# Delta heads traced with a tile between producer and reader, an adaLN closing in two jobs, one pool of four PSUM banks

## The chip, the cores and the metric

One core of a Trainium2 chip runs the kernel. The metric is the device time of one execution in microseconds (us); lower is better. A time "before" is the median of three runs; a profile is one execution taken by the hardware profiler.

## What is computed

A trunk of two layers over 512 latent and 256 context tokens of width 2048. Each layer modulates and normalises its input with shift, scale and gate vectors that come from `silu(c) @ ada_w + ada_b` (adaLN, 2048 to 6144, once for the latents' condition and once for the context's), runs one combined input projection of 6480 columns, and feeds three head groups: four retention heads, four gated Delta heads, eight latent-attention heads. All are gated, joined by one output projection and added to the residual.

```python
h = rmsnorm(x, norm_w[i]) * (1.0 + scale[:, None]) + shift[:, None]
zl = split_cols(h @ w_in[i], IN_SPLITS)
# gated DeltaNet, per head of 128:
qkv = silu(centred_dwconv(concat([q, k, v]), conv_w))   # 5 taps
q = l2norm(q) * 128 ** -0.5;  k = l2norm(k)
# S_t = a_t (I - b_t k_t k_t^T) S_{t-1} + b_t k_t v_t^T,  o_t = S_t^T q_t, both directions
```

## The kernel before

Tokens lie along the free dimension: a tile is 128 features by 768 tokens, context first (256), then latents (512). A projection of 128 columns (`proj`, L290, through `proj_in`, L363) takes 16 row blocks of 128; the weights come from HBM in four loads, are split into a high and a low float32r part (`wh` on ACT, L227; `wl` on VectorE, L228; four buffers each of four row blocks), and every row block gives three products, each one matmul over the latents (`zl`, L284) and one over the context (`zc`, L286). The result is evicted from PSUM by `evac` (L369): the context half on VectorE (L371), the latent half on ACT (L372).

A layer has three phases. Phase A makes all input projections and runs the Delta and retention heads. Phase B is the attention, phase C the output projection. Which instruction stands where on an engine is fixed when the program is built: the order in the source is a priority, and the framework lays each engine's queue by that priority and by its own estimate of when operands and buffers are ready. The chip then works each queue in order. So a reader may be placed too early for the chip, and then its engine waits.

`gdn_head(h, gs)` (L756) is one Delta head. `conv_in` (L737) takes a projection, evicts it to `cz`, makes the five-tap convolution `cy` (an ACT copy, L744, and eight steps on VectorE, L751) and a SiLU (`ce`, L392 to L396, L400). It does this for the query (`qT`), the key (`kr`) and the value (`vT`). Behind the query come its squares (`lsq`, ACT, L763) and the sums of these by small matmuls (`ss`, L767). Behind the key come the transposes by TensorE (`knp`, `turn`, L661), the norm's rsqrt from sums of squares (`token_rstd`, L650), the scaled key `kn` (L664), and its transposes back (`ktp`) that are copied to `kT`. The value is turned in `vnp` (L787). In the source each of these readers stands right behind what it reads: `ss` behind the query's squares, then the key's `conv_in`, then `knp`, `ktp`, then the value's `conv_in`, then `vnp`. In head 0 the gate's projection (`gate`, L618) stands between the value and `vnp`. Then follow the decay masks, the triangular inverse (`vtp`, `xp`, `rp`, `xrp`) and the scan of six steps in both directions (`chain`, from L908), and `out_norm` (`osq`, `ot`).

The head is a long row of dependent steps. What covers them is a list `fill` of other projections (latents for the attention `cq`, `ckv`, gates `gg`, `mg`, retention inputs `rr`), of which so many are emitted behind each head (`nf`, L1057), with lower priority for coming later. The order by hand is in these lines:

```python
fill = cq + gg[1:2] + ckv + gg[2:3] + rr[0] + gg[3:] + rr[1] + rr[2] + rr[3] + mg
nf = [7, 6, 4, 5, 3, 3, 4, 4]
for i, n in enumerate(nf):
    (gdn_head if i < 4 else ret_head)(*((i, gs) if i < 4 else (i - 4,)))
    for f in fill[sum(nf[:i]):sum(nf[:i + 1])]:
        f()
```

The query, key and value of head 0 are projected before phase A (`first_groups`, L319), so its three `conv_in` find their sums ready.

The adaLN vectors that are not needed at the start are made in 64 jobs, one in the middle of each projection of phase A of layer 0 and in its phase C (`ada_job`, L510). A job loads a part of `ada_w`, scales it on ACT (`ada_p`, L474) and sums it on GpSimd (`ada_a`, L476; eight additions of 128x512). After every four jobs, the next job closes a group (`ada_close`, L492): eight small matmuls into `ada_z` (L497), a copy to `ada_e` by ACT (L501), and behind it at once four matmuls that read `ada_e` into `ada_q` (L504) and an addition on VectorE (L505).

PSUM has three kinds of tiles: `pz` (tag `z`, one bank, 3 of them: all `zl`, `zc`, `ada_z`, `ada_q`, the attention's transposes `ptp` and values `vz`), `pm` (tag `m`, two banks, 2 of them) and `pc` (tag `ch`, one bank, 1 of them: the scan's first direction `chain`, the attention's sums `oacc` and the first adaLN sums).

Of the kernel before, what the change touches and what calls it, by code (L numbers as in the profile page):

```python
# [11 lines left out]
F32 = mybir.dt.float32  # L12
# [8 lines left out]
P = 128  # L21
# [11 lines left out]
C_GDN = 2048  # L33
# [68 lines left out]
def trunk(  # L102
# [16 lines left out]
    ps = ctx.enter_context(tc.tile_pool(name="ps", bufs=1, space=PSUM))  # L119
    dr = ctx.enter_context(tc.tile_pool(name="dr", bufs=1, space=DRAM))  # L120

    def pz(name="z"):
        return ps.tile([P, 512], F32, name=name, tag="z", bufs=3)

    def pm(name="m"):
        return ps.tile([P, 1024], F32, name=name, tag="m", bufs=2)

    def pc(name="ch"):
        return ps.tile([P, 512], F32, name=name, tag="ch", bufs=1)

    def lslot(name, dt=F32R):
        return lp.tile([P, NT], dt, name=name, tag="L")
# [3 lines left out]
    def w_(tag, name, dt=F32, n=NT):  # L136
        return wk.tile([P, n], dt, name=name, tag=tag, bufs=BUFS[tag])

    mk = lambda name: w_("t", name)
# [61 lines left out]
    def col_params(parts, n, name, alloc=None, queue=None):  # L201
        st = mk("pst")
        V.memset(st[:, :P], 0.0)
        o = 0
        for ap in parts:
            r = ap.shape[0] // P
            (queue or dma)(out=st[o:o + r, :P], in_=rows(ap))
            o += r
        p_ = pz("pst_ps")
        T.transpose(p_[:, :P], st[:, :P], ident)  # L210
        d = alloc(name)[:, :n] if alloc else fixed(n)
        V.tensor_copy(d, p_[:, :n])
        return d
# [149 lines left out]
    def proj_in(l, c0, hs, need_ctx):  # L363
        if (l, c0) in ready:
            return ready.pop((l, c0))
        segs, m = in_segs(l, c0)
        return proj(segs, hs, m, need_ctx, True)

    def evac(dst, zl, zc, m=P, scale=1.0):  # L369
        if zc is not None:  # L370
            V.tensor_scalar(out=dst[:m, 0:NX], in0=zc[:m, :NX], scalar1=scale, scalar2=None, op0=ALU.mult)  # L371
        S.activation(out=dst[:m, NX:NT], in_=zl[:m], func=AF.Copy, scale=scale)  # L372
# [25 lines left out]
    def silu_mul(dst, src, e):  # L398
        sigmoid(e, src)
        V.tensor_tensor(out=dst, in0=src, in1=e, op=ALU.mult)  # L400
# [30 lines left out]
    def ada_scale(l, n0, n):  # L431
        if 16 <= n0 < 32:
            k0 = n0 - 16
            V.tensor_scalar(out=s1[l][:, k0:k0 + n, :], in0=ada_t[l][:, n0:n0 + n, :],
                            scalar1=1.0, scalar2=None, op0=ALU.add)
            V.tensor_tensor(out=s1[l][:, k0:k0 + n, :], in0=s1[l][:, k0:k0 + n, :],
                            in1=par[l, 0][:, 48 + k0:48 + k0 + n].unsqueeze(2).to_broadcast([P, n, 2]), op=ALU.mult)
# [24 lines left out]
    ada_state = {}  # L462
# [20 lines left out]
    def ada_run(job):  # L483
        l, s, qd = job
        if qd == 0:
            ada_accs.append(wk.tile([P, 2, 256], F32, name="ada_a", tag="ada_a", bufs=3))
        for i in range(2):
            ada_quad(l, s, qd + i, ada_accs[-1])
        if qd and s % 2:
            ada_state[1] = (l, 2 * s - 2)  # L490

    def ada_close(l, n0):  # L492
        z = pz("ada_z")[:, :256]
        for i, acc in enumerate(ada_accs):
            for v in range(2):
                g = 2 * i + v
                T.matmul(z[32 * g:32 * g + 32], lhsT=ones[:, :32], rhs=acc[:, v], start=True, stop=True,  # L497
                         tile_position=(0, 32 * g))
        ada_accs.clear()
        e = wp.tile([P, 256], F32, name="ada_e", tag="ada_e", bufs=2)  # L500
        S.copy(e, z)  # L501
        q = pz("ada_q")
        for j in range(2):
            T.matmul(q[:, 4 * j:4 * j + 4], lhsT=e[:, j * P:(j + 1) * P], rhs=sel4, start=True, stop=True)  # L504
        V.tensor_tensor(out=ada_t[l][:, n0:n0 + 4, :].rearrange("p (i j) v -> p i j v", j=2),  # L505
                        in0=q[:, :8].rearrange("p (j i v) -> p i j v", j=2, i=2),
                        in1=par[l, 0][:, n0:n0 + 4].rearrange("p (i j) -> p i j", j=2).unsqueeze(3).to_broadcast([P, 2, 2, 2]), op=ALU.add)
        ada_scale(l, n0, 4)

    def ada_job():  # L510
        if 1 in ada_state:
            ada_close(*ada_state.pop(1))
        job = next(ada_jobs, None)
        if job:
            ada_run(job)
# [91 lines left out]
    def phase_a(l, hs):  # L607
        last = l == DEPTH - 1
        parB = par[l, 1]
        if True:  # L610
# [7 lines left out]
            def gate(c0, j):  # L618
                lo_ctx = not last
                zl, zc = proj_in(l, (c0), hs, lo_ctx)  # L620
                z, e = ev("gz"), ev("ge")
                lo = 0 if lo_ctx else NX
                evac(z, zl, zc)
                silu_mul(z[:, lo:], z[:, lo:], e[:, lo:])
                dma(out=gate_d[l][j][:, lo:], in_=z[:, lo:])
# [24 lines left out]
            def token_rstd(src, c0, sq, fill_v):  # L650
                ss, y, t = tiny("nss"), tiny("nry"), tiny("nrt")
                for n in range(c0, NCH):
                    S.activation(out=sq[:, n * P:(n + 1) * P], in_=src[:, n * P:(n + 1) * P], func=AF.Square,
                                 accum_out=ss[:, n:n + 1])
                fill_v(ss[:, c0:])
                rsqrt(ss[:, c0:], y[:, c0:], t[:, c0:])
                return ss

            def turn(dst, src, c0):
                for n in range(c0, NCH):  # L660
                    T.transpose(dst[:, n * P:(n + 1) * P], src[:, n * P:(n + 1) * P], ident)  # L661

            def scale_tokens(dst, src, r, c0):
                V.tensor_tensor(out=c6(dst)[:, c0:], in0=c6(src)[:, c0:],  # L664
                                in1=r[:, c0:].unsqueeze(2).to_broadcast([P, NCH - c0, P]), op=ALU.mult)
# [71 lines left out]
            def conv_in(dst, c0, grp, need_ctx):  # L737
                zl, zc = proj_in(l, c0, hs, need_ctx)
                z = ev("cz")
                lo = 0 if need_ctx else NX  # L740
                evac(z, zl, zc)
                y = mk("cy")
                w = lambda j: parB[:, 12 * j + grp:12 * j + grp + 1]
                S.activation(out=y[:, lo:NT], in_=z[:, lo:NT], func=AF.Copy, scale=w(2))  # L744
                for j in (0, 1, 3, 4):
                    o = j - 2
                    for a, b in ((0, NX), (NX, NT)):
                        if a < lo:
                            continue
                        a_, b_ = max(a, a - o), min(b, b - o)  # L750
                        V.scalar_tensor_tensor(out=y[:, a_:b_], in0=z[:, a_ + o:b_ + o], scalar=w(j),  # L751
                                               in1=y[:, a_:b_], op0=ALU.mult, op1=ALU.add)
                e = mk("ce")
                silu_mul(dst[:, lo:NT], y[:, lo:NT], e[:, lo:NT])

            def gdn_head(h, gs):  # L756
                be, gcol, egl, ekd, nbe = gs
                qT = pt("qT")
                qlo = NX if last else 0
# [1 line left out]
                qv = tiny("qv")  # L761
                sq = mk("lsq")
                S.activation(out=sq[:, qlo:NT], in_=qT[:, qlo:], func=AF.Square)  # L763
                m = pm("ss")
                c0 = qlo // P
                for n in range(c0, NCH):
                    T.matmul(m[:, n:n + 1], lhsT=sq[:, n * P:(n + 1) * P], rhs=ones[:, 0:1], start=True, stop=True)  # L767
                V.tensor_scalar(out=qv[:, c0:], in0=m[:, c0:NCH], scalar1=EPS, scalar2=EPS * HD, op0=ALU.add, op1=ALU.mult)
                kr = mk("kr")
                conv_in(kr, C_GDN + 512 + h * P, 4 + h, True)  # L770
                kT, kn = pt("kT"), pt("kn")
                m = pm("knp")
                turn(m, kr, 0)
                r = token_rstd(m, 0, kr, lambda ss: V.tensor_scalar(out=ss, in0=ss, scalar1=EPS, scalar2=None, op0=ALU.add))
                scale_tokens(kn, m, r, 0)
                m = pm("ktp")
                turn(m, kn, 0)
                S.copy(kT, m[:, :NT])
                vT = mk("vT")
                conv_in(vT, C_GDN + 1024 + h * P, 8 + h, True)  # L780
                if h == 0:
                    gate(C_GDN + 1536, 4)

                vn = pt("vn")
                m = pm("vnp")
                for n in range(NCH):
# [261 lines left out]
            gs = kr_ab()  # L1048
# [4 lines left out]
            gg = [lambda h=h: gate(C_GDN + 1536 + h * P, 4 + h) for h in range(4)]  # L1053
            mg = [lambda j=j: gate(C_MG + j * P, 8 + j) for j in range(8)]
            mg.insert(6, lambda: pair_groups(l, (C_MG + 6 * P, C_MG + 7 * P), hs, not last))
            fill = cq + gg[1:2] + ckv + gg[2:3] + rr[0] + gg[3:] + rr[1] + rr[2] + rr[3] + mg
            nf = [7, 6, 4, 5, 3, 3, 4, 4]  # L1057
            for i, n in enumerate(nf):
                (gdn_head if i < 4 else ret_head)(*((i, gs) if i < 4 else (i - 4,)))
                for f in fill[sum(nf[:i]):sum(nf[:i + 1])]:  # L1060
                    f()

    def phase_b(l):
# [313 lines left out]
```

## Time and profile before

| | us |
|---|---|
| median of three runs | 3215.6 |
| the three runs | 3215.6, 3217.71, 3211.18 |
| the profiled execution | 3222.98 |
| its span, first to last instruction | 3221.2 |
| TensorE busy in it | 3053.8 |
| VectorE / ACT / GpSimd busy in it | 2031.1 / 1657.0 / 697.1 |

PE is TensorE, DVE VectorE, ACT ScalarE, POOL GpSimd, SP the engine that issues the transfers; L661 is line 661 of the kernel. In a row of waits the instruction left of `<-` waited for the one right of it. In a timeline a bracket gives the idle time of that engine before the instruction and what ended it. A row by stretches gives a stretch, its length, each engine's busy time with its number of instructions, TensorE's granted clock as a share of 2.4 GHz, the transfers' share and GB/s.

### The profile page before, as it was taken

The page shows a single profiled execution, that of the slowest core. Times are in us where ns is not written, and L with a number is a line of the kernel's source. Part 1 is how long each engine was busy: PE and PEld are TensorE (multiplying, and loading weights), DVE is VectorE, ACT ScalarE, POOL GpSimd, SP SyncE. Part 2 cuts the span into 40 slices and gives each one's busy share as a digit, 9 for nine tenths or more (in the row PEclk, how much of TensorE's full clock was granted, in tenths as well). Part 3 has the DMA queues.
Part 4 walks back from the last instruction along what each step waited for, and adds up shares of the span by engine and source line. Part 5 has one row for each costly group of instructions (what it writes and reads, how often), then busy time and mean ns, then how long its engine had stood idle before and what let it go on. Part 6 is the DMA issues. An engine that isn't in the chain of part 4 may idle for free.

```text
span 3221.2 us, 50805 instructions
## 1 busy us (share of the span) xinstructions
PE 3053.8 (95%) x18925; PEld 2589.3 (80%) x18925; DVE 2031.1 (63%) x3524; ACT 1657.0 (51%) x3492; POOL 697.1 (22%) x487
## 2 busy tenths in 40 slices
PE   6998989989889999999999999999999999999998
PEld 3576878878778878899888888888898888888887
DVE  3269568477577566766763355867585767766644
ACT  3266555654555656544677645442424245544534
POOL 0036344443443544000268700000000000000000
PEclk8999999989999999999999999999999999999999
DMA  8763433423424545512465542322323256512444
GB/s 286 257 193 115 122 103 99 133 66 92 134 79 141 159 144 159 159 48 60 136 216 164 160 122 66 98 72 61 102 58 99 74 149 186 147 54 62 134 118 129
DMA packets 496655, 399.22 MB, mean 124 GB/s; under 512 B 45367, under 2 KB 433047, under 8 KB 496407
## 3 DMA queue, kind: packets, MB, share of 16 engines
q1 hardware_dynamic: 496083, 395.87, 41.5%
q8 instruction: 148, 2.42, 0.3%
q14 instruction: 101, 0.82, 0.1%
q0 software_dynamic: 96, 0.02, 0.0%
q10 hardware_dynamic: 227, 0.08, 0.0%
HBM read 340.90 MB, written 54.97 MB: 123 GB/s over the span
## 4 chain that ended last, share of the span: by engine, by line
PE 53%; POOL 2%; ACT 2%; DMA 2%; DVE 2%; issue 1%; SPq 0%; ACTq 0%; POOLq 0%; DVEq 0%
PE zl L284 21%; PE zlc L284 7%; PE zc L286 5%; PE vz L267 4%; PE sc L1157 3%; POOL ada_a L476 2%; PE oacc L1216 2%; PE zt L275 2%; PE zlc L286 1%; PE ptp L1209 1%; PE racc L1037 1%; DMA araw<-in_ada_w_dram 1%; PE f L284 1%; ACT ada_p L474 1%; DMA gb<-g_d 0%
## 5 line engine op out<-in xcount | busy, mean ns | idle before, releaser
L476 POOL TENSOR_TENSOR ada_a<-ada_a,ada_p 128x512 f32<-128x512 f32 x480 | 695.1, 1448 | 1144.8 <-ACT ada_p L474 1098.7
L228 DVE TENSOR_TENSOR wl<-raw,wh 128x512 fp32r<-128x512 f32 x632 | 486.3, 771 | 421.2 <-ACT wh L227 333.1
L227 ACT CAST wh<-raw 128x512 fp32r<-128x512 f32 x632 | 377.8, 605 | 562.0 <-PE zc L286 208.3
L284 PE MATMUL zl<-hh,wh 128*128 128x512 f32 (+1 forms) x1440 | 581.4, 404 | 1.9 <-ACT hh L227 1.8
L284 PE MATMUL zl<-hl,wh 128*128 128x512 f32 (+1 forms) x1440 | 581.3, 404 | 1.0 <-DVE hl L228 1.0
L284 PE MATMUL zl<-hh,wl 128*128 128x512 f32 (+1 forms) x1440 | 581.3, 404 | 0.0
L474 ACT ACTIVATE ada_p<-araw,const_f 128x256 f32<-128x256 f32 x960 | 423.4, 501 | 64.7 <-DMA araw<-in_ada_w_dram 41.3
L284 PEld LDWEIGHTS zl<-hh,wh 128*128 128x128 f32 (+1 forms) x1440 | 274.0, 190 | 64.9 <-issue 3.8
L284 PEld LDWEIGHTS zl<-hh,wl 128*128 128x128 f32 (+1 forms) x1440 | 274.1, 190 | 58.6 <-issue 1.1
L284 PEld LDWEIGHTS zl<-hl,wh 128*128 128x128 f32 (+1 forms) x1440 | 273.8, 190 | 58.6 <-DVE hl L228 2.5
L286 PE MATMUL zc<-hh,wh 128*128 128x256 f32 (+1 forms) x960 | 279.6, 291 | 6.1 <-ACT ce L372 4.9
L286 PE MATMUL zc<-hl,wh 128*128 128x256 f32 (+1 forms) x960 | 277.9, 289 | 0.0
L286 PE MATMUL zc<-hh,wl 128*128 128x256 f32 (+1 forms) x960 | 277.8, 289 | 0.0
L286 PEld LDWEIGHTS zc<-hh,wh 128*128 128x128 f32 (+1 forms) x960 | 183.8, 191 | 14.6 <-ACT ce L372 6.7
L286 PEld LDWEIGHTS zc<-hh,wl 128*128 128x128 f32 (+1 forms) x960 | 184.3, 192 | 3.4 <-issue 2.9
L286 PEld LDWEIGHTS zc<-hl,wh 128*128 128x128 f32 (+1 forms) x960 | 184.5, 192 | 2.6 <-issue 0.8
L284 PE MATMUL zlc<-mh,wl 128*128 128x512 f32 x448 | 178.6, 399 | 0.0
L284 PE MATMUL zlc<-mh,wh 128*128 128x512 f32 x448 | 178.0, 397 | 0.0
L284 PE MATMUL zlc<-ml,wh 128*128 128x512 f32 x448 | 177.3, 396 | 0.0
L751 DVE SCALAR_TENSOR_TENSOR cy<-cz,const_f,cy 128x511 f32<-128x511 f32 (+3 forms) x176 | 141.8, 859 | 17.8 <-ACT cy L744 17.3
L284 PEld LDWEIGHTS zlc<-mh,wh 128*128 128x128 f32 x448 | 84.9, 189 | 20.4 <-ACT ada_p L474 0.8
L284 PEld LDWEIGHTS zlc<-ml,wh 128*128 128x128 f32 x448 | 84.8, 189 | 19.0
(1250 smaller groups left out, 6419.3 us busy)
## 6 DMA issues: line engine op xcount, KB each, us to landing
raw<-in_w_in_dram SPq DMA_DIRECT2D x368, 256.0 KB, 3.6
araw<-in_ada_w_dram SPq DMA_DIRECT2D x256, 256.0 KB, 3.4
raw<-in_w_out_dram SPq DMA_DIRECT2D x144, 256.0 KB, 3.8
ar<-in_ada_w_dram SPq DMA_DIRECT2D x128, 256.0 KB, 5.1
x_d<-xt SPq DMA_DIRECT2D x32, 384.0 KB, 3.6
raw<-in_w_in_dram SPq DMA_DIRECT2D x72, 128.0 KB, 3.4
ret_d<-rw SPq DMA_DIRECT2D x20, 384.0 KB, 2.8
rz<-ret_d SPq DMA_DIRECT2D x20, 384.0 KB, 3.5
```

The costliest lines, as they stand in the source:

```text
L227: S.copy(hi, src)
L228: V.tensor_tensor(out=lo, in0=src, in1=hi.bitcast(F32), op=ALU.subtract)
L267: T.matmul(z[:, 256 * i:256 * i + 256], lhsT=x_[:, (j + i) * P:(j + i + 1) * P], rhs=w, start=first and k == 0 and i == 0, stop=end and k ...
L275: T.matmul(z, lhsT=w, rhs=xx[:, a:b], start=own and first and k == 0, stop=own and last and k == nk - 1)
L284: T.matmul(zl[:m], lhsT=w, rhs=xx[:, NX:], start=st, stop=sp)
L286: i = T.matmul(zc[:m, :NX], lhsT=w, rhs=xx[:, :NX], start=st and zc_open, stop=sp and zc_open)
L474: S.activation(out=pr[:, v], in_=raw[:, i, :], func=AF.Copy, scale=cs32[:, 2 * k + v:2 * k + v + 1])
L476: G.tensor_tensor(out=acc, in0=acc, in1=pr, op=ALU.add)
L751: V.scalar_tensor_tensor(out=y[:, a_:b_], in0=z[:, a_ + o:b_ + o], scalar=w(j), in1=y[:, a_:b_], op0=ALU.mult, op1=ALU.add)
L1037: T.matmul(acc[:, :NL], lhsT=a[:, sl], rhs=b[:, :NL], start=st and i == 0, stop=sp and i == NCH - 1)
L1157: T.matmul(m[:, po:po + n], lhsT=a[:, qs], rhs=b[:, ko:ko + n], start=i == 0, stop=i == len(ops) - 1)
L1216: T.matmul(acc[:, os], lhsT=a[:, sl], rhs=b[:, js], start=j == 0 and n == 0, stop=j == nk - 1 and n == 2)
```

## The change

Three edits. First, `gdn_head` takes one more argument, `between`, and its readers move: the key's `conv_in` stands before the query's `ss`, the value's `conv_in` before the key's `knp`, and `between()`, one projection, before `ktp`. In head 0 it is the gate that stood in the head before; in heads 1 to 3 it is the first of the head's own fills (one of `ckv`, then two of the retention inputs), which are one fewer behind the head. Second, the closing of an adaLN group is cut in two: `ada_close` ends with the copy to `ada_e`, and the matmuls into `ada_q` with what follows are `ada_turn`, called at the beginning of the next `ada_job`. Third, `pc` draws on the tag `z`, which has four banks in place of three and one.

```diff
     def pz(name="z"):
-        return ps.tile([P, 512], F32, name=name, tag="z", bufs=3)
+        return ps.tile([P, 512], F32, name=name, tag="z", bufs=4)
...
     def pc(name="ch"):
-        return ps.tile([P, 512], F32, name=name, tag="ch", bufs=1)
+        return ps.tile([P, 512], F32, name=name, tag="z", bufs=4)
...
         S.copy(e, z)
+        return l, n0, e
+
+    def ada_turn(l, n0, e):
         q = pz("ada_q")
...
     def ada_job():
+        if 2 in ada_state:
+            ada_turn(*ada_state.pop(2))
         if 1 in ada_state:
-            ada_close(*ada_state.pop(1))
+            ada_state[2] = ada_close(*ada_state.pop(1))
...
-            def gdn_head(h, gs):
+            def gdn_head(h, gs, between):
...
                 S.activation(out=sq[:, qlo:NT], in_=qT[:, qlo:], func=AF.Square)
+                kr = mk("kr")
+                conv_in(kr, C_GDN + 512 + h * P, 4 + h, True)
                 m = pm("ss")
...
-                kr = mk("kr")
-                conv_in(kr, C_GDN + 512 + h * P, 4 + h, True)
+                vT = mk("vT")
+                conv_in(vT, C_GDN + 1024 + h * P, 8 + h, True)
                 kT, kn = pt("kT"), pt("kn")
                 m = pm("knp")
                 turn(m, kr, 0)
...
                 scale_tokens(kn, m, r, 0)
+                between()
                 m = pm("ktp")
                 turn(m, kn, 0)
                 S.copy(kT, m[:, :NT])
-                vT = mk("vT")
-                conv_in(vT, C_GDN + 1024 + h * P, 8 + h, True)
-                if h == 0:
-                    gate(C_GDN + 1536, 4)
-
                 vn = pt("vn")
...
-                (gdn_head if i < 4 else ret_head)(*((i, gs) if i < 4 else (i - 4,)))
-                for f in fill[sum(nf[:i]):sum(nf[:i + 1])]:
+                mine = fill[sum(nf[:i]):sum(nf[:i + 1])]
+                if i < 4:
+                    gdn_head(i, gs, gg[0] if i == 0 else mine.pop(0))
+                else:
+                    ret_head(i - 4)
+                for f in mine:
                     f()
```

## Rows read from the trace of the kernel before

**Rows 1.** The page: span, busy time by engine, GpSimd's forty slices.

```profile
span 3221.2 us, 50805 instructions
...
PE 3053.8 (95%) x18925; PEld 2589.3 (80%) x18925; DVE 2031.1 (63%) x3524; ACT 1657.0 (51%) x3492; POOL 697.1 (22%) x487
...
POOL 0036344443443544000268700000000000000000
```

**Rows 2.** TensorE's waits, 400 to 1000 us: total us, times, longest.

```profile
PE knp L661 <- DVE kr L400: 17.5, 3, 6.0
PE ss L767 <- ACT lsq L763: 16.6, 3, 5.7
PE vtp L852 <- DVE vt L846: 6.4, 5, 2.6
PE ot L661 <- DVE osq L664: 6.0, 2, 4.6
...
PE vnp L787 <- DVE vT L400: 1.9, 1, 1.9
```

**Rows 3.** TensorE's waits, whole span.

```profile
PE ada_q L504 <- ACT ada_e L501: 14.9, 7, 3.9
...
PE zc L286 <- ACT ce L372: 4.9, 2, 2.9
```

**Rows 4.** Timeline, Delta head 1, layer 0: start us, us, instruction, idle before.

```profile
413.27 0.42 DVE L371 TENSOR_SCALAR cz<-zc 128x256 f32<-128x256 f32 x1 [3.33 <-PE zc L286]
...
430.83 0.96 DVE L400 TENSOR_TENSOR qT<-cy,ce 128x768 f32<-128x768 f32 x1 [0.98 <-ACT ce L396]
...
439.71 0.42 DVE L371 TENSOR_SCALAR cz<-zc 128x256 f32<-128x256 f32 x1 [3.02 <-PE zc L286]
...
441.75 7.80 DVE L751 SCALAR_TENSOR_TENSOR cy<-cz,const_f,cy 128x254 f32<-128x254 f32 x6 [0.97 <-ACT cy L744]
...
457.50 0.96 DVE L400 TENSOR_TENSOR kr<-cy,ce 128x768 f32<-128x768 f32 x1 [0.98 <-ACT ce L396]
...
432.78 1.87 PE L767 MATMUL ss<-const_f,lsq 128*128 128x1 f32 x8 [5.36 <-ACT lsq L763]
...
458.60 0.87 PE L661 MATMUL knp<-const_f,kr 128*128 128x128 f32 x3 [6.00 <-DVE kr L400]
```

**Rows 5.** Low-clock stretches: length, busy us, clock; sums of front (7), `ada_q` (5).

```profile
483.00:486.40 3.40, 3.40 (x18) 3.40 (x18) 3.40 (x6) 2.01 (x4) 2.53 (x3) 0.51 0.04 5
...
sum 51.00, PE 35.91 PEld 33.04 DVE 20.96 ACT 28.95 POOL 12.18; mean PE 5.13 PEld 4.72 DVE 2.99 ACT 4.14 POOL 1.74
...
704.90:708.30 3.40, 3.40 (x13) 2.80 (x12) 1.77 (x2) 1.68 (x4) 0.00 (x0) 0.50 0.00 0
...
sum 20.40, PE 20.21 PEld 17.30 DVE 7.22 ACT 11.23 POOL 10.23; mean PE 4.04 PEld 3.46 DVE 1.44 ACT 2.25 POOL 2.05
```

**Rows 6.** Timeline of TensorE in and after a low-clock stretch (220.2-227.0).

```profile
225.04 0.41 PE L286 MATMUL zc<-hh,wl 128*128 128x256 f32 x1
...
225.68 0.41 PE L286 MATMUL zc<-hh,wh 128*128 128x256 f32 x1
...
228.07 0.28 PE L286 MATMUL zc<-hh,wl 128*128 128x256 f32 x1
...
228.42 0.28 PE L286 MATMUL zc<-hh,wh 128*128 128x256 f32 x1
```

**Rows 7.** Timeline of SP's queue in head 1.

```profile
447.60 17.76 SPq L240 DMA_DIRECT2D raw<-in_w_in_dram  x4
```

**Rows 8.** Busy time in 362.0-413.2, 590.0-637.2, 809.5-842.3 us together.

```profile
sum 131.20, PE 129.88 PEld 110.49 DVE 48.06 ACT 80.04 POOL 58.51; mean PE 43.29 PEld 36.83 DVE 16.02 ACT 26.68 POOL 19.50
```

**Rows 9.** Timeline of VectorE in Delta head 2, layer 1.

```profile
2304.75 0.43 DVE L371 TENSOR_SCALAR cz<-zc 128x256 f32<-128x256 f32 x1 [3.25 <-PE zc L286]
...
2306.51 3.26 DVE L751 SCALAR_TENSOR_TENSOR cy<-cz,const_f,cy 128x254 f32<-128x254 f32 x6 [0.74 <-ACT cy L744]
...
2316.50 0.96 DVE L400 TENSOR_TENSOR kr<-cy,ce 128x768 f32<-128x768 f32 x1 [0.91 <-ACT ce L396]
```

## The prediction

> **What bounds the kernel now.** I read the page first: TensorE is busy for 3053.8 of 3221.2 us, VectorE, at 2031.1, is not near that, and GpSimd, which does nothing but the adaLN sums, works in the slices of layer 0 alone [rows 1]. So this is a matmul stream with holes, and only holes in it are to be won. The second view, TensorE's waits, says which holes [rows 2]: in the stretch of Delta heads 1 to 3 of layer 0 the longest two are the transposes of the key (`knp`, waiting for `kr`, 17.5 us in three waits) and the column sums of the query (`ss`, waiting for `lsq`, 16.6 us in three); one `vnp` behind the value adds 1.9. In the whole run `ada_q` waits 14.9 us in seven places for `ada_e`, and a projection's context half waits 4.9 us in two places for the eviction that frees its bank [rows 3].
>
> The third view shows why a front waits [rows 4]. In head 1 the query projection's eviction begins at 413.27 and `qT` is made at 430.83 + 0.96; TensorE has nothing placed between but part of the key projection, and stands at `ss` for 5.36 us until 432.78. The key does the same: eviction at 439.71, `kr` at 457.50 + 0.96, `knp` at 458.60 after 6.00 us. From eviction to use it is 19.5 us for the query and 18.9 us for the key. Heads 2 and 3 repeat this (the three waits each of rows 2).
>
> Each hole also costs afterwards: in the stretches behind these waits the granted clock is 0.50 or 0.51, the lower level (1.2 GHz), and TensorE worked 35.9 us in them behind the front's waits and 20.2 us behind those of `ada_q` [rows 5]. A latent and a context matmul follow each other every 0.64 us there and every 0.35 us after [rows 6], so 45% of such time is lost.
>
> **The change part by part.** All sums are against the profiled execution, 3222.98 us with its 3221.2 us span; that is 7.4 us above the median of the three runs, and I take the gain off the median. No matmul, weight load or conversion is added or removed; only places, waits and banks change.
>
> *1. The front of heads 1 to 3 in layer 0.* `ss` now comes behind the whole key projection, `knp` behind the value's, `ktp` behind one fill. A projection is 48 such pairs (16 row blocks, 3 products), so 48 x 0.35 = 16.8 us of cover. `ss` needs 19.5: up to 2.7 us stay, less if a few matmuls of an adaLN closing fall inside; I take 2.0, three times: 6.0. `knp` is reached after the rest of `ss`, its twelve small matmuls and 16.8 us, about 20 against 18.9: nothing. `vnp` has a projection and two sets of transposes before it, also nothing. Removed: 17.5 + 16.6 + 1.9 = 36.0 of idle and 0.45 x 35.9 = 16.2 at the low clock, 52.2 in all; less 6.0, less 2.3 for half of the low-clock time that such short waits could leave (the `vnp` wait of 1.9 us left 3.4 us [rows 5]; three times 3.4 x 0.45 is 4.6). **43.9 us**, between 39 (2.7 three times and all 4.6) and 52. Who is queued behind these readers: behind `ss` the value projection, and `qv`, which only the norm at the head's end reads; behind `knp` the squares, `kn`, `ktp` and so the whole chain. The chain is not late for it: a projection of the front now takes 26.4 us from eviction to eviction [rows 4], and would take about 19, so that three of them end sooner, the last of the three being a fill that is then done.
>
> *2. The moved fill.* It is the same projection, with its eviction, its job and one store. On SP it goes ahead of loads that are themselves paced by free buffers: four loads took 17.76 us to issue [rows 7]. If its store stands behind them, one of four `ev` buffers is held that long; the other three carry the convolutions. Cost 0, at worst part of such a wait once per head, since the loads run a projection ahead. On GpSimd nothing passes anything: jobs keep their order. After the chains 131.2 us of fills are left over in heads 0 to 2, 129.9 of them TensorE work [rows 8], so taking one fill forward uncovers no chain. Head 0 has its projections already finished, so `ss` there keeps its wait: 0.
>
> *3. The closing in two.* `ada_q` reads `ada_e` one job later, at least half a projection (8.4 us) behind a copy that was late by 2.1 us in the mean of seven. All 14.9 us go, and 0.45 x 20.2 = 9.1 at the low clock: **24.0 us**. The ACT copy and its GpSimd sums keep their places; `ada_z` holds its bank no longer than before. The values are read by a later phase, and calls enough remain to flush the last.
>
> *4. The pool of four.* The two waits for eviction, 4.9 us, and one stretch of low clock like the single one shown in rows 5 (3.4 x 0.45 = 1.5) come to at most 6.4 us if a fourth bank is free then (the chain's bank is, before the chain begins); none if it isn't. I take half, **3.2**. In the attention the sums and the projections share what they had, 3 + 1 banks: 0, bounded by one eviction wait of 2.5 us (4.9 / 2) either way per sum.
>
> *5. Waits that stay.* `vtp` (6.4) and `ot` (6.0) in the same heads [rows 2] come from VectorE being later than the order of the queues supposes. With front idle gone VectorE gets less slack, and they are laid anew: from 12.4 gained to 12.4 lost. I take half the loss, **-6.2**. Layer 1 has no GpSimd work [rows 1]: 0.
>
> Sum: 43.9 + 24.0 + 3.2 - 6.2 = 64.9 us. 3215.6 - 64.9 = **3151 us**. Its own ends: 39 + 24 + 0 - 12.4 = 51 and 52.2 + 24 + 6.4 + 12.4 = 95, so 3121 to 3165.
>
> **Rivals.** *(a) The producers stretch.* The first six convolution steps of the key take 7.80 us in head 1 of layer 0, beside GpSimd's sums, and 3.26 us in layer 1, where there are none; the whole way from eviction to `kr` is 18.7 against 12.7 us [rows 4, 9]. If TensorE passes a projection every 18 instead of 26 us, all eight sums of a job could fall into one convolution. The two steps outside that six would go at 1.30 us (7.80 / 6) instead of 0.54 (3.26 / 6), +1.5, and two more two-input operations of 0.96 us, stretched in the same proportion, +2.7: 4.2 us. Then `ss` waits 6.2 instead of 2.0, three times, +12.6; `knp` still comes behind, since that wait delays it as well; and waits of this length, like the seven of the front with 35.9 us at the low clock, lose 2.3 us each there, +6.9 less the 2.3 already in the sum. Together +17: 3168. By the Trainium skill ("SBUF — State Buffer", section "Who interferes with whom") VectorE's second SBUF input and GpSimd's reads use one interface under an exclusive lock, so denser sums lengthen exactly these steps. By that rule this rival would be the case, and the two durations of rows 4 and 9 agree with it.
>
> *(b) The order doesn't move.* The emission order is a priority, and a reader is placed where its operands were supposed ready: 14.1 us after the eviction in head 1. If a projection's weights are supposed late, `ss` slips in ahead of them as now. Then only parts 3 and 4 pay: 3215.6 - 27.2 = 3188. Against it: weights come from four buffers of four blocks, a projection ahead.
>
> *(c) Slower: the chain starves for a bank.* The chain's first direction had a bank for itself; now two projections can hold four, and a step may wait for one to end, 16.8 us. Five waiting steps in a head are 84 us, of which the fills left over hide 131.2 / 3 = 43.7; 40 bare us in each of three heads, 3151 + 121 = 3272. It turns slower than before from about 3.9 waits per head. Against it: projections follow one another, so two hold banks together only for an eviction, whose two waits were 4.9 us.
>
> *(d) Nothing moves*, because another engine takes up what TensorE gains: 3216. Against it: VectorE is busy for 63% of the span [rows 1].
>
> **How the numbers follow.** Forecast 0.54, (a) 0.17, (b) 0.12, (c) 0.11, (d) 0.06. Measurement tells 0.2%, about 6 us, from no change: faster is the first three, 0.83; same 0.06; slower 0.11. The likeliest case's middle is 3151. The range reaches from the forecast's low end, about 3120, over (a) to (b) with a little for its bounds, 3194; (c), (d) and thin ends stay out.
>
> **What would show it.** Right: `ss` waits of 0 to 3 us and `knp` of none in heads 1 to 3 of layer 0, `ada_q` gone from the waits, TensorE's time at the low clock down by more than half, and its busy time by some 25 us with equal instruction counts (less work at the low clock). Wrong in part 1: `ss` or `knp` again about 5 us, with convolutions longer than 8 us for (a), or with a reader in the midst of a projection for (b). For (c): `chain` matmuls waiting for an eviction by ACT, and new idle before `kkp`. The prediction is wrong if `vtp` and `ot` grow by more than 12 us.

## The result, and the profile after

The changed kernel takes **3626.17 us** in the median of four runs (3621.34 to 3633.19); the kernel before took 3216.25 us in four (3211.18 to 3217.71). The ratio is 1.1274, its 95% interval 1.1256 to 1.1292: 13% slower, where 3151 us were forecast. The profiled execution took 3621.34 us. One execution each of e7 and e9 below took 5875 and 6134 us; it counts in neither ratio, and the trace of e7 is of it, so no time is read from that trace.

The head of the page after, with TensorE's slices, their granted clock and the transfers' GB/s:

```profile
span 3619.6 us, 50726 instructions
## 1 busy us (share of the span) xinstructions
PE 3153.8 (87%) x18925; PEld 2683.9 (74%) x18925; DVE 2024.4 (56%) x3524; ACT 1658.6 (46%) x3492; POOL 701.5 (19%) x487
...
PE   7947995986968999999998975978969699999998
PEclk8967996996979999999999995988979799999999
...
GB/s 288 260 108 50 140 108 30 141 104 29 141 57 92 182 148 155 141 53 65 221 157 152 138 61 4 117 51 56 85 19 104 14 110 157 167 93 56 111 121 127
```

Each engine of the page has as many instructions as before [rows 1]. TensorE is busy 100.0 us longer (3153.8 against 3053.8) and idle for 465.8 us instead of 167.4, which together are the 398.4 us that the span grew. The slices show where: four notches in each layer, one per Delta head, with TensorE busy for four to seven tenths, in most of them a lower clock, and few transfers (in five of them 30, 29, 4, 19 and 14 GB/s).

TensorE's waits after, whole span:

```profile
PE vtp L848 <- DVE Xt L836: 61.2, 11, 8.1
PE vtp L855 <- DVE vt L849: 59.5, 32, 2.2
PE xp L871 <- DVE vt L868: 40.5, 32, 1.6
PE xrp L897 <- DVE R L893: 29.7, 32, 1.2
PE knp L666 <- DVE kr L400: 27.0, 3, 16.3
PE ktp L666 <- DVE kn L669: 25.8, 4, 14.5
...
PE chain L928 <- ACT vnew L926: 7.3, 20, 0.5
```

Where the list before was led by the front's readers [rows 2, 3], it is now led by every step of the triangular inverse (`vtp`, `xp`, `xrp`), each waiting for the step on VectorE before it: 32 waits, that is four in each of eight heads. The chain of the Delta head has nothing beside it. Busy time by stretches says the same. Each stretch is one head of layer 0, up to about the sums of its norm (`ot`). Before, it begins at about the first products of keys (`kkp`); after, it begins at about the last projection ahead of them, 13.6 and 3.5 us sooner than `kkp` in the two heads shown. Two of the four heads are shown and the sum of all four, TensorE's matmuls of line 284 (latent halves of projections) alone; first before, then after:

```profile
254.00:362.00 108.00, 65.85 (x172) 33.28 (x171) 0.97 0.34 98
484.00:590.00 106.00, 63.30 (x170) 32.67 (x170) 0.97 0.33 94
...
sum 407.00, PE 212.54 PEld 108.49; mean PE 53.13 PEld 27.12
```

```profile
238.00:345.00 107.00, 8.96 (x23) 4.73 (x23) 0.68 0.09 14
536.00:640.00 104.00, 9.97 (x25) 5.11 (x24) 0.71 0.12 30
...
sum 408.00, PE 28.02 PEld 14.38; mean PE 7.01 PEld 3.59
```

What is gone from beside the chain is the projections: 28.02 us of these matmuls instead of 212.54. They run afterwards. The chain gains little from having TensorE to itself: from the first `kkp` to the first `ot`, timed alike in both, the four heads take 368.3 us together, 410.5 before.

The timeline of TensorE in head 1 of layer 0 shows when they stop and when they come back:

```profile
536.02 0.28 PE L286 MATMUL zc<-hh,wl 128*128 128x256 f32 x1
536.96 0.85 PE L666 MATMUL ktp<-const_f,kn 128*128 128x128 f32 x6 [0.65 <-DVE kn L669]
538.78 0.88 PE L790 MATMUL vnp<-const_f,vT 128*128 128x128 f32 x6 [0.97 <-DVE vT L400]
539.49 1.54 PE L820 MATMUL kkp<-kT 128*128 128x128 f32 x12
...
601.53 0.49 PE L919 MATMUL chain<-vn,Xt 128*128 128x128 f32 x2 [0.65 <-DVE Xt L901]
...
621.72 0.71 PE L915 MATMUL chain<-St,kT 128*128 128x128 f32 x4
622.19 0.48 PE L284 MATMUL zl<-hh,wh 128*128 128x512 f32 x1
```

From 536.30 to 622.19 no projection runs. The scan begins at 601.53, and 621.72 is the first matmul of its sixth and last step, the one that opens the sixth `chain` tile. The first projection follows 0.47 us later. In all eight heads it is so (328.20 and 328.67, 884.28 and 884.75, 1126.87 and 1127.33 in layer 0; 2260.39 and 2260.53 in the first of layer 1, and the other three likewise). Counted from the timeline, with the projections of line 267 included, the holes are 122.6, 85.9, 88.9, 83.6, 111.1, 76.1, 75.0 and 81.6 us: 724.7 us. In the heads of the kernel before there is none of over 12 us.

The projections were not waiting on the chip. Their row on the page has 7.4 us of idle time before it in the whole run:

```profile
L284 PE MATMUL zl<-hh,wh 128*128 128x512 f32 (+1 forms) x1440 | 575.5, 400 | 7.4 <-DVE cz L371 4.1
```

They stand behind the scan in TensorE's queue, and that queue is laid when the program is built. Its order alone shows it: in TensorE's order before, at most 18 matmuls of inverse and scan stand between two matmuls of projections; after, there are eight places with 360 to 392. Nor were the banks in use: from 541 to 601 us there is one last eviction of a projection (`ce`) and, of tiles of the pool, not a matmul.

### The profile page after: what moved, and what is told of

The parts are those of the page before. It is cut to its first block, busy times and chain, and to the rows that moved or that the text cites. A ratio compares the mean times of both kernels' runs of the same rounds, so it can differ in the third digit from the quotient of the medians.

```text
span 3619.6 us, 50726 instructions
## 1 busy us (share of the span) xinstructions
PE 3153.8 (87%) x18925; PEld 2683.9 (74%) x18925; DVE 2024.4 (56%) x3524; ACT 1658.6 (46%) x3492; POOL 701.5 (19%) x487
## 5 line engine op out<-in xcount | busy, mean ns | idle before, releaser
L228 DVE TENSOR_TENSOR wl<-raw,wh 128x512 fp32r<-128x512 f32 x632 | 473.3, 756 | 611.3 <-ACT wh L227 513.7
L284 PE MATMUL zl<-hh,wh 128*128 128x512 f32 (+1 forms) x1440 | 575.5, 400 | 7.4 <-DVE cz L371 4.1
L284 PE MATMUL zl<-hh,wl 128*128 128x512 f32 (+1 forms) x1440 | 571.5, 397 | 0.0
L284 PE MATMUL zl<-hl,wh 128*128 128x512 f32 (+1 forms) x1440 | 570.4, 396 | 0.8 <-DVE hl L228 0.8
L227 ACT CAST wh<-raw 128x512 fp32r<-128x512 f32 x632 | 369.7, 603 | 388.6 <-PE zc L286 133.3
L286 PE MATMUL zc<-hh,wh 128*128 128x256 f32 (+1 forms) x960 | 271.6, 283 | 0.0
L756 DVE SCALAR_TENSOR_TENSOR cy<-cz,const_f,cy 128x511 f32<-128x511 f32 (+3 forms) x176 | 149.3, 904 | 18.1 <-ACT cy L749 17.7
L877 ACT COPY X<-xtp 128x768 f16<-128x768 f16 x32 | 25.6, 799 | 249.9 <-PE xtp L876 249.9
L926 ACT COPY vnew<-chain 128x128 f32<-128x128 f32 x80 | 20.8, 266 | 185.1 <-DVE vd L922 180.1
```

The source lines that it names most:

```text
L227: S.copy(hi, src)
L228: V.tensor_tensor(out=lo, in0=src, in1=hi.bitcast(F32), op=ALU.subtract)
L284: T.matmul(zl[:m], lhsT=w, rhs=xx[:, NX:], start=st, stop=sp)
L286: i = T.matmul(zc[:m, :NX], lhsT=w, rhs=xx[:, :NX], start=st and zc_open, stop=sp and zc_open)
```

## The experiments

The theories, by the letters that the expectations use. **O**, order: a pool hands out its tiles in the order of the source, so a fill's projection, which stands behind the scan in the source, gets no bank until the scan's six tiles have been opened. **R**: the reordered head has taken the cover away. **C**: a pool of four is too small for both. **D** and **M** concern what the waits of the front do, and come at the end.

| run | what is in it | median us | ratio to before, interval |
|---|---|---|---|
| after | all three edits | 3626.17 | 1.1274, 1.1256 to 1.1292 |
| e1 | after with pools apart | 3190.57 | 0.9939, 0.9922 to 0.9955 |
| e2 | before with the pool of four | 3724.55 | 1.1600, 1.1576 to 1.1623 |
| e3 | before with the reorder | 3206.43 | 0.9983, 0.9973 to 0.9993 |
| e4 | before with the closing in two | 3205.38 | 0.9987, 0.9976 to 0.9997 |
| e5 | after, one scan tile asked for early | 3226.38 | 1.0056, 1.0036 to 1.0077 |
| e6 | after, one scan tile asked for late | 3525.0 | 1.0987, 1.0965 to 1.1009 |
| e7 | after, scan in the two-bank pool | 3209.97 | 0.9994, 0.9983 to 1.0006 |
| e8 | e1, `ss` behind the value | 3181.54 | 0.9913, 0.9896 to 0.9930 |
| e9 | e8, two fills in the front | 3208.27 | 0.9990, 0.9981 to 0.9999 |
| e10 | e8 again, beside e9 | 3185.6 | 0.9917, 0.9902 to 0.9931 |

### Which of the three edits

**e1**, after with the old pools:

```diff
 def pz(name="z"):
-    return ps.tile([P, 512], F32, name=name, tag="z", bufs=4)
+    return ps.tile([P, 512], F32, name=name, tag="z", bufs=3)
...
 def pc(name="ch"):
-    return ps.tile([P, 512], F32, name=name, tag="z", bufs=4)
+    return ps.tile([P, 512], F32, name=name, tag="ch", bufs=1)
```

Expected: 

> The changed kernel with its two pools apart again (three banks for projections, one for the scan and the attention's sums); the reordered head and the divided closing stay. Theory O (the pool hands out its tiles in the order of the source, so a fill's projection waits until the scan's six tiles, which stand ahead of it, have been opened): the holes of 80 us and more without a projection matmul in the inversion of each Delta head go, and what the prediction counted for parts 1, 3 and 5 remains: 3216 - (43.9 + 24.0 - 6.2) = 3154 us, 3125 to 3170. Theory R (the reordered head itself takes the cover away, as one fill is brought forward and the head's other work gets ahead of the fills): about 3600 us, holes as in the changed kernel.

Measured: 3190.57 us, and no hole as after in any head (at most 18 matmuls of inverse and scan between two of projections). O has the holes right; the time lies above its range, for reasons taken up below. **e2**, the kernel before with the pool edit alone (the two `+` lines of the change):

Expected: 

> The kernel before with the pool of four banks alone. Theory O: all eight heads lose the cover of their inversion, as in the changed kernel, which stands 472 us above the 3154 us expected without the pool: 3216 + 472 = 3690 us, 3600 to 3720. Theory R: 3216 us, within 10 us, no holes.

Measured: 3724.55 us, 16% slower than before, with eight holes of 89.4 to 122.7 us; the time is just above O's range of 3600 to 3720. So the pool alone makes the loss and R falls. In e2 the readers of the front stand bare too, `vnp` first of all; this row, the first of TensorE's waits there, is what the reorder takes out again in the kernel after, where `vnp` waits 1.2 us:

```profile
PE vnp L787 <- DVE vT L400: 84.6, 8, 16.1
```

**e3**, the reorder alone, and **e4**, the closing alone, both on the kernel before:

Expected: 

> The kernel before with the reordered head alone. Theory O: parts 1 and 5 of the prediction, 3216 - 43.9 + 6.2 = 3178 us, 3165 to 3190; ss waits of 2 to 3 us in heads 1 to 3 of layer 0, no knp wait. Theory R: above 3500 us.

Expected: 

> The kernel before with the divided closing alone. Both theories: part 3 of the prediction, 3216 - 24.0 = 3192 us, 3188 to 3200; ada_q gone from TensorE's waits. If the waits only move on to the next instruction, 3216.

Measured: 3206.43 and 3205.38 us, beside 3211.22 us for the kernel before on the same chip, about 5 us less each. Neither costs anything, and neither pays what was forecast; that is taken up below.

### Order or size

**e5** keeps the one pool of four, but the scan's first direction takes a single tile, asked for at the head's front, where `ss` is, which also moves from its two-bank tile into this one:

```diff
-                m = pm("ss")
+                m = one = pc("one")
...
-                        p_ = pc("chain") if d == 0 else pm("chain")[:, :512]
+                        p_ = one if d == 0 else pm("chain")[:, :512]
```

**e6** is the same, but asks for the tile right ahead of the scan, behind the inverse:

```diff
                 St, seen = [None] * 2, set()
+                one = pc("one")
...
-                        p_ = pc("chain") if d == 0 else pm("chain")[:, :512]
+                        p_ = one if d == 0 else pm("chain")[:, :512]
```

Expected: 

> The changed kernel, but the scan's first direction uses one tile of the pool of four for all its six steps, and that tile is asked for and first written by the head's ss, before the key. Theory O (tiles of a pool are handed out in the order of the source): nothing of the pool is asked for between the head's front and its fills, so the fills go into the inversion again: no stretch of over 30 us without a projection matmul in a head, 3190 us (as with the pools apart), 3170 to 3230. Theory C (the pool is simply too small: scan and projections take one another's banks): a bank is now held through the whole head, so slower than the changed kernel, over 3626 us.

Expected: 

> The same single tile, asked for right before the scan, where the changed kernel asks for the first of six. Theory O: fills may start with the scan's first step instead of its last ones, some 20 us earlier in a hole of 84 to 123 us; the inversion before it stays bare: 3626 - 8 x 20 = 3466 us, 3430 to 3530, holes of 60 to 100 us. Theory C: as when it is asked early, since it holds one bank in either case.

Measured: 3226.38 and 3525.0 us. In e5 a bank is held through the whole head, from `ss` to the end of the scan, and the time is 0.6% above before: by C it would have been the worst of all. The longest stretch without a projection in a head is 29.9 us. In e6 the pool is held much less, and the time is 9.9% above. TensorE's timeline of e6 in head 1 of layer 0, at the end of its hole:

```profile
588.57 2.87 PE L891 MATMUL rp<-Xt,A 128*128 128x128 f32 x12
591.23 0.43 PE L920 MATMUL one<-vn,Xt 128*128 128x128 f32 x2
591.42 0.48 PE L284 MATMUL zl<-hh,wh 128*128 128x512 f32 x1
591.73 0.28 PE L286 MATMUL zc<-hh,wh 128*128 128x256 f32 x1
```

The projections come back 0.19 us behind the first matmul that writes `one`, not behind the sixth step as in the kernel after. So the hole ends where the last tile asked for ahead of the fills is opened. Through the scan, projections and steps then run beside each other with that bank held. The holes of e6 are 100.6, 67.3, 64.2, 63.6, 88.7, 55.3, 55.7 and 59.8 us, 555.2 us in all. That is 169.5 us less than after, 21.2 in a head; in the kernel after, it took 20.2 us in head 1 from the scan's first matmul to the opening of its last tile (601.53 to 621.72). The stretch of head 1's inverse in e5, and the hole of e6 there, all engines:

```profile
488.00:594.00 106.00, 92.17 (x713) 77.83 (x711) 86.14 (x153) 56.39 (x131) 45.45 (x31) 0.94 0.30 86
```

```profile
524.00:591.00 67.00, 28.03 (x282) 25.02 (x282) 51.63 (x91) 16.51 (x29) 12.71 (x8) 0.59 0.11 32
```

TensorE works 92.17 of 106 us at a clock of 0.94 in the one, 28.03 of 67 us at 0.59 in the other. In TensorE's order, at most 27 matmuls of inverse and scan stand between two of projections in e5, 280 to 302 at eight places in e6. O stands and C falls.

**e7** takes the scan out of the pool of four; its first direction uses the two-bank tiles, as the second always did. The attention's sums stay in the pool.

```diff
-                        p_ = pc("chain") if d == 0 else pm("chain")[:, :512]
+                        p_ = pm("chain")[:, :512]
```

Expected: 

> The changed kernel with both directions of the scan in the two-bank tiles, so that the pool of four serves projections, the adaLN sums and the attention's sums alone. Theory O: no fill waits, no holes; against the pools apart a bank is won (some 3 us of waits for eviction) and the scan loses one of three buffers: 3190 us, 3180 to 3215. Theory C: the attention's sums still share, so some of the loss stays, above 3250 us.

Measured: 3209.97 us. At most 18 matmuls of inverse and scan stand between two of projections, as before. The 13% are gone with the scan's tiles alone, so the attention's sums in the pool do no such harm. But by the ratios it is 0.55%, some 18 us, behind e1 and about even with before. Whether the two-bank tiles of the scan or the shared pool elsewhere cost these was not separated.

### What the front and the closing are worth

**e8** is e1 with the query's sums (`ss` and its VectorE step) moved behind the value's `conv_in`:

```diff
                 conv_in(kr, C_GDN + 512 + h * P, 4 + h, True)
+                vT = mk("vT")
+                conv_in(vT, C_GDN + 1024 + h * P, 8 + h, True)
                 m = pm("ss")
...
-                vT = mk("vT")
-                conv_in(vT, C_GDN + 1024 + h * P, 8 + h, True)
```

Expected: 

> The pools apart, and in each Delta head ss stands behind the value's projection, not behind the key's. In the run with the pools apart ss waited 2.2, 2.4 and 2.5 us in heads 1 to 3 of layer 0. If a tile of distance more takes these away and nothing takes their place: 7 us and some 4 us of low clock, 3190 - 11 = 3180 us. If the next reader waits in its stead (knp, whose distance shrinks by the sums), 3190 us.

**e9** puts one more of the head's own fills ahead of the key's transposes; **e10** is e8 beside it on the same chip:

```diff
-            def gdn_head(h, gs, between):
+            def gdn_head(h, gs, between, ahead):
...
+                ahead()
                 kT, kn = pt("kT"), pt("kn")
                 m = pm("knp")
...
-                    gdn_head(i, gs, gg[0] if i == 0 else mine.pop(0))
+                    gdn_head(i, gs, gg[0] if i == 0 else mine.pop(0), mine.pop(0))
```

Expected: 

> Reader given distance (theory D): in Delta heads 1 to 3 of layer 0 the waits of the key's transposes (knp, 16.1 us in three in the kernel with the sums behind the value) go, since one more projection of 16.8 us stands ahead of them; about 16 us and some low-clock time less, 3165 (3155 to 3172). Waits only move on (theory M, as in the closing alone): knp falls under 5 us, but 8 us or more turn up at the next readers (kkp, qkp, vtp, ot) or behind the chain, whose cover is one fill shorter: 3175 to 3190.

Expected: 

> The kernel with the sums behind the value once more, so that the second fill in the front is compared with it on one chip: 3181 (3175 to 3188) under both theories.

Measured: e8 3181.54 and e10 3185.6 us, both 0.8 to 0.9% under before, the lowest medians of the study and below both kernels of the case; e9 3208.27 us. TensorE's waits from 400 to 1000 us, Delta heads 1 to 3 of layer 0, in e1, e8 and e9 in turn:

```profile
PE vtp L855 <- DVE vt L849: 9.0, 5, 2.9
PE ss L774 <- ACT lsq L768: 7.1, 3, 2.5
PE kkp L820 <- ACT kT L786: 6.1, 2, 5.8
PE ot L666 <- DVE osq L669: 5.1, 3, 3.5
PE zc L286 <- ACT rw L372: 4.4, 1, 4.4
PE knp L666 <- DVE kr L400: 4.4, 2, 3.2
...
PE qkp L829 <- ACT vn L791: 3.5, 1, 3.5
```

```profile
PE knp L666 <- DVE kr L400: 16.1, 3, 5.6
```

```profile
PE ada_z L497 <- DVE kn L669: 12.7, 1, 12.7
```

TensorE's waits for the norm's sums at the heads' ends, whole span, in e10 and in e9:

```profile
PE ot L666 <- DVE osq L669: 10.6, 10, 4.0
```

```profile
PE ot L666 <- DVE osq L669: 23.2, 14, 4.1
```

In e8 `ss` has left the list and `knp` is back at nearly what it was [rows 2], and yet the ratio is some 0.25% below that of e1, about 8 us. The intervals of the two overlap a little (0.9922 to 0.9930), and where the gain lies, if there is one, these rows don't say: the time is that of the first case expected, the waits are those of the second. In e9 `knp` is gone from the list, as D had it, and the kernel is about 23 us behind e10: one wait of 12.7 us has come in its place, and over the run `ot` waits 23.2 us in fourteen places, 10.6 in ten in e10. M has the direction; the measured time lies above its range of 3175 to 3190. That the second fill had covered more behind the chains than it covers in the front fits the `ot` rows, which stand at the chains' ends, but it was not tried by itself.

## Why the prediction was wrong

**The step that failed is part 4.** It said of the fourth bank that the chain's bank is free "before the chain begins", and of the attention that sums and projections "share what they had, 3 + 1 banks: 0". It counted banks. A pool has an order too: the fills stand behind the scan in the source and were always taken forward beside the inverse, since they had a pool of their own; with the scan's tiles in the same pool they can't be. Part 4 has +3.2 us gained; e2 has 513 us lost (3724.55 - 3211.22), and in the full change, where the reorder covers the fronts, pools apart bring some 430 us (by the ratios, 1.1274 and 0.9939).

**Rival (c)** had the place, the shared bank, and the wrong victim. It let the scan wait for a projection, priced at up to 84 us in a head less what the fills hide. The scan waits for no eviction of a projection: its largest sum of waits after is 7.3 us, in twenty waits, for its own `vnew`, and the four heads of layer 0 take 368.3 us from `kkp` to `ot`, 410.5 before. It is the projections that are held back, and with them goes the inverse's cover. So where rival (c) had the direction right, it was by another road. The line of the prediction that would have shown (c), "`chain` matmuls waiting for an eviction", showed nothing; new idle before `kkp` came, 11.6 us in four waits, but for `kT`. The sign set for a wrong prediction came too: the first two `vtp` rows after have 120.7 us, where `vtp` and `ot` were to grow by 12 at most. The evidence could have been read ahead: rows 8 put the leftover fills behind the chain at 131.2 us, and the rest of the fills thus ran beside it, ahead of scan tiles that the source asks for first.

**Part 1, the front: right at its places, wrong in its sum.** In e1 `ss` keeps 2.18, 2.41 and 2.54 us in heads 1 to 3 (forecast 2.0 each) and `knp` 4.4 in two (forecast none). So 36.0 us of idle time became 11.5 there. But the reorder by itself pays 5 us, not some 38 (43.9 less part 5's 6.2). What failed is the step that says whom the removed waits uncover: "The chain is not late for it". In e1 `kkp` waits 6.1 us for `kT`, `qkp` 3.5 for `vn`, a projection 4.4 for an eviction. `kkp` and `qkp` stand next in line behind the front and got no tile between. In e3, the reorder alone, 11 us of the front's 36.0 are left, and `vtp` (6.4 before [rows 2]), `ada_q` (5.2 before) and `qkp` have grown; TensorE's waits there from 400 to 1000 us:

```profile
PE ada_q L504 <- ACT ada_e L501: 9.6, 2, 5.2
PE vtp L850 <- DVE vt L844: 9.1, 5, 2.9
PE ss L769 <- ACT lsq L763: 8.0, 3, 2.8
...
PE qkp L824 <- ACT vn L786: 4.2, 1, 4.2
PE knp L661 <- DVE kr L400: 2.2, 2, 1.4
```

**Part 2, the moved fill at 0**, was not tried alone. The second fill moved in e9 cost about 23 us, so the reason given, that taking one forward uncovers no chain, is doubtful for the next one.

**Part 3, the closing: 24.0 forecast, about 5 measured.** In phase A its three waits of `ada_q` (7.0 us) are gone in e4, while `vnp` grows from 1.9 to 5.8 us and `zc` from 4.9 to 7.2. In phase C nothing is gained. TensorE's waits from 1590 to 1900 us, the first row before, then those in e4:

```profile
PE ada_q L504 <- ACT ada_e L501: 8.0, 4, 3.9
```

```profile
PE zlc L284 <- ACT ada_e L501: 3.3, 1, 3.3
PE zlc L284 <- DVE wl L228: 2.4, 3, 1.1
PE ada_q L507 <- ACT ada_e L501: 1.5, 1, 1.5
...
PE zlc L284 <- ACT wh L227: 0.9, 3, 0.4
```

The four of e4 are 8.1 us. Two of them wait for weight parts that ACT and VectorE make: what TensorE needs next from them is late as well. The step that failed is "All 14.9 us go": a wait was taken for that of one reader, and by these rows what its engine owed next was late as well.

**Part 5** gave the waits laid anew 12.4 us at most. Between 200 and 1260 us of e1, the waits that went or shrank come to 41.6 us (`knp` 12.4, `ss` 9.2, `ada_q` 7.0, `zc` for `ce` 4.1 the largest) and those that are new or grew to 29.8 (`kkp` 6.1, `vtp` for `vt` 5.1, `qkp` 3.5, `zc` for `rw` 3.2). So 72% came back, and TensorE's busy time in this stretch is 974.35 us, only 11.4 more than the 962.93 of before. In e3 it is 40.2 us and 31.3. These are single executions, and the one before lies 7.4 us above its median, so the sums hold to some us only.

**The other rivals.** (a), the stretched producers, holds in its direction and not in its size: in head 1 the six steps of the key's convolution take 8.43 us in e1, 7.80 before [rows 4], and the query's 7.79 against 7.78. Over the whole way from eviction to `kr`, where 4.2 us were priced, it is 19.1, 18.5 and 19.2 us in heads 1 to 3 of e1, 18.7, 18.4 and 18.7 before. `ss` does not feel it; `knp`, whose producer it is, waits 3.2 us there. The Trainium skill ("SBUF — State Buffer", section "Who interferes with whom") would have such steps lengthen beside GpSimd's sums; the trace agrees, for GpSimd is busy for 7.81 us beside the key's six steps, 7.15 before, and for 7.14 beside the query's, 7.13 before. (b), the order doesn't move, fell: `ss` of head 1 stands behind the key projection's last matmul in e1 (439.55), where before it stood within that projection (432.78). (d), nothing moves, is near what e3 and e4 measure of parts 1 and 3, with 0.17% and 0.13%. Without the pool the direction would have been right and the size not: e1 is 0.6% faster, which off 3215.6 us is 3196, just above the range's upper end of 3194.

**The clock** followed the idle time, as the prediction had it. In the bare stretches after, TensorE is busy for 32 to 51 of 80 us, and the mean granted clock lies between its two levels (1.00 and 0.50), in the last almost at the lower; in the heads of before it was 0.97:

```profile
560.00:640.00 80.00, 50.79 (x401) 43.12 (x402) 45.83 (x89) 13.39 (x41) 0.00 (x0) 0.73 0.09 21
...
2160.00:2240.00 80.00, 31.80 (x286) 28.75 (x287) 58.53 (x115) 19.18 (x36) 0.00 (x0) 0.52 0.02 7
```

The projections themselves took no longer (575.5 us for the row above, 581.4 before). With their durations added up by tile, it is the Delta heads' small matmuls that take longer, at equal counts: `chain` 205.1 us instead of 166.0, `rp` 75.3 instead of 49.7, `vtp` 62.5 instead of 50.7. These three add 76.5 us, most of the 100.0 us of added busy time.

## What to carry to other kernels

Before you let two kinds of tile share a pool, write down in which order the source asks for them, and ask which of them the queue takes ahead of that order now: it won't any more, and free banks don't help. If they must share, ask for one long-lived tile early and keep it (3226 us) rather than late (3525 us for one tile, 3626 for six); apart, as in e1, they took 3191. And price a removed wait only after asking what the same producing engine owes next: here, of 41.6 us removed in the Delta and retention heads, 11.8 stayed removed in that execution.

## What was not expected of the hardware

Holding one bank of four from a head's front to the end of its scan (e5) costs little: 0.6% over before and, by the ratios, 1.2% over e1. Three banks then carried the projections, as before, and no run here shows a gain from a fourth. Part of the cost stands where the tile is asked for: in the first head of each layer TensorE waits 17.0 and 11.1 us there for `lsq`, where `ss` of e1 waits 5.2 and 1.4. That the early request held projections back there too, as the late ones do, fits this but was not tried. The row of the whole span:

```profile
PE one L774 <- ACT lsq L768: 35.3, 5, 17.0
```

Removing `knp`'s three waits (16 us) made the kernel slower by about 23 us (e9 and e10). The wait of 12.7 us that came in is put down to VectorE's `kn`, although the matmul reads the GpSimd sums `ada_a`; what really ended it stays open.
